# Conditioning tiles on GpSimd's queue, the first scale and shift on TensorE, and six blocks in two halves of k tiles

## Chip, cores and metric

One core of one Trainium2 chip runs the whole kernel in one launch. The metric is device microseconds, lower is better. Engines are named as in the profile: PE is TensorE (matmul), PEld its weight load, DVE is VectorE, ACT is ScalarE, POOL is GpSimd, and SP is SyncE, which here only issues transfers.

## The reference, cut to what matters

```python
def mod(h, shift, scale):        # modulate
    return h * (1 + scale) + shift

c_act = silu(c)                                       # one row of 1024
for i in range(2):
    # 9 rows of 1024 for each layer: shift, scale and gate of three sublayers
    sh0, sc0, g0, sh1, sc1, g1, sh2, sc2, g2 = split(c_act @ mod_w[i] + mod_b[i], 9)
    h = mod(rms_norm(x, norm_g[i, 0]), sh0, sc0)
    x = x + 0.5 * g0 * swiglu(h, ffn_w_gu[i, 0], ffn_w_down[i, 0])
    h = mod(rms_norm(x, norm_g[i, 1]), sh1, sc1)
    x = x + g1 * (pool_mixer(h) if i == 0 else diff_attention(h))
    h = mod(rms_norm(x, norm_g[i, 2]), sh2, sc2)
    x = x + 0.5 * g2 * swiglu(h, ffn_w_gu[i, 1], ffn_w_down[i, 1])
return rms_norm(x, final_g)
```

`x` has 256 tokens of 1024 channels, `w_gu` is 1024 x 5632 (gate and up), `w_down` 2816 x 1024. Everything is float32.

## The kernel before, in words

The channels lie on partitions: `xT` holds `x` as eight k tiles of 128 channels by 256 tokens. There are four FFNs, a pooling mixer after the first and attention after the third.

**Products.** A float32 operand is split into two parts that TensorE takes at its fast rate, `hi` (rounded, ScalarE, L313) and `lo` (the rest, VectorE, L314). Three matmuls, `hi*hi`, `hi*lo` and `lo*hi` (`prod3`, L333 to L335), stand for one product. The activations are split in the same way (`hh`, `hl`). A *weight unit* is 512 rows by 256 columns (512 KB, 24 matmuls); `split_unit` loads it into one of five `raw` buffers from SyncE's queue (L310) and splits it into one of six `hi` and `lo` buffers. `unit()` keeps four units in advance. A *block* is 256 output columns in one PSUM bank: two units.

**Conditioning.** `mod_w` is stored so that a tile of 128 outputs by 1024 inputs (512 KB) is loaded into one of three `cond` buffers, also from SyncE's queue (L268), and VectorE multiplies it with the row `cact` and sums along it (`gemv_tile`, L276). There are 144 such tiles. All but the first 16 are background work: `Background.tick` puts them between the blocks of the FFNs, by the lists `UP` and `DOWN`.

**The start.** The first FFN needs shift and scale of its own sublayer first. The loop takes k tile by k tile: two conditioning tiles give scale and shift of 128 channels, ScalarE and VectorE make `hh` and `hl` of that k tile (L840 to L847), and two narrow units (one k tile of 768 gate columns and one of 768 up columns, 384 KB each) feed it into six blocks that stay open in PSUM, `early`. After eight k tiles the six blocks are complete.

**Order.** Each engine runs its instructions in the order in which the scheduler put them, and so does each issuing queue: a transfer that waits for a buffer holds those behind it. The scheduler picks the order from priorities and its own idea of durations; `issue_after` keeps work behind a given instruction.

At the end of an FFN the residual is added (VectorE, L396), ScalarE squares it, and VectorE sums the squares into `acc` (L407). TensorE needs `acc` (L377) soon after it has begun the next FFN, whose first blocks run on the unnormalised values `xh`, `xl` (L431 to L433).

Of the kernel before, what the change touches and what calls it, by code (L numbers as in the profile page):

```python
# [11 lines left out]
F32 = mybir.dt.float32  # L12
# [23 lines left out]
EARLY = 3  # L36
# [26 lines left out]
def weight_units():  # L63
# [49 lines left out]
def lay_out(inputs):  # L113
# [11 lines left out]
    for name, ix in weight_units():  # L125
# [7 lines left out]
        "c": np.ascontiguousarray(w["c"]),  # L133
        "mod_w": np.ascontiguousarray(w["mod_w"].transpose(0, 2, 1)),
# [8 lines left out]
def trunk(ctx: ExitStack, tc: tile.TileContext, x, c, mod_w, small, weights, diff_lambda, k_rope, out):  # L143
# [72 lines left out]
    for half in range(2):  # L216
        hs = slice(half * KD // 2, (half + 1) * KD // 2)
        nc.sync.dma_start(xT[:, hs, :], x[:, hs, :])
    nc.sync.dma_start(cact, c.broadcast_to([P, D]))
# [7 lines left out]
    warm(AF.Silu, eps1)  # L227
    with tc.high_priority(offset=1000):
        S.activation(cact, cact, AF.Silu)
    warm(AF.Abs_reciprocal_sqrt, cact[:, 0:1])  # L230
# [26 lines left out]
    tiles = iter([(0, p, k) for k in range(KD) for p in (1, 0)] + [(*part, k) for part in PARTS for k in range(KD)])  # L257
    loaded = []

    def gemv_load(n):  # L260
        while len(loaded) < n:
# [6 lines left out]
            nc.sync.dma_start(raw, mod_w[i, r0:r0 + P, :])  # L268
# [33 lines left out]
    place = [0]  # L302

    def split_unit(nk, n):
# [7 lines left out]
        with tc.high_priority(offset=-400):  # L312
            S.activation(hi[:, :w], raw[:, :w], AF.Copy)  # L313
            V.tensor_tensor(lo[:, :w], raw[:, :w], hi[:, :w].bitcast(F32), ALU.subtract)  # L314
# [491 lines left out]
    xr = [t1k(1024, "qk", 2) for _ in range(2)]  # L806
    with tc.high_priority(offset=1000):
        pt = psmall()
        for half in range(2):
            sq = t1k(1024, "u", U_BUFS)  # L810
# [3 lines left out]
        idle = psmall()  # L814
        for _ in range(WARM):
            PE.matmul(idle[:, :P], ones, ones, start=True, stop=True)
# [7 lines left out]
    with tc.high_priority(offset=1000):  # L824
        scaled_x(0, 1)

    early = [psum2(), psum2()] + [psum() for _ in range(2 * EARLY - 2)]
    b1, d = const([P, KD], "b1"), const([P, 2, KD], "d")  # L830
# [5 lines left out]
    def scale_and_shift(k):  # L836
# [89 lines left out]
```

## Time and profile before

| | |
|---|---|
| median of three runs | 946.21 us (945.92 to 951.72) |
| profiled execution | 958.03 us, span of its instructions 956.2 us |
| granted TensorE clock over the span | 0.981 |
| PE / DVE / ACT / POOL busy | 913.8 / 742.8 / 502.4 / 0.7 us |
| transfers | 238.18 MB, mean 249 GB/s; SyncE's queue 236.88 MB of it |

"x" with a number counts instructions, "<-" between names stands between what is written and what is read, and a "<-" in brackets or behind a bar names what ended the idle time. `Lnnn` is a line of the kernel; a helper's line collects the work of all that call it.

### The profile page before, as it was taken

To read this page: it belongs to the slowest core of one execution; us is meant where nothing else is said; L and a number is where in the kernel's file an instruction comes from. 1 tells how busy PE (TensorE), PEld (TensorE's weight loads), DVE (VectorE), ACT (ScalarE), POOL (GpSimd) and SP (SyncE) were. 2 spreads that over 40 slices of the span, in tenths; PEclk is the share of its full clock that TensorE was granted. 3 is DMA by queue.
4 is the path that set the end of the run, shared out by engine and by line. 5 is a ranking of instruction groups with operands and counts; after the bars stand their busy time and mean duration, and the time that the engine had idled before them with its cause. 6 is when DMAs were issued, how large, how long until landed. Compare 5 with 4: busy or idle time off the path is not lost.

```text
span 956.2 us, 18740 instructions
## 1 busy us (share of the span) xinstructions
PE 913.8 (96%) x7532; PEld 900.8 (94%) x7532; DVE 742.8 (78%) x1211; ACT 502.4 (53%) x771; POOL 0.7 (0%) x6
## 2 busy tenths in 40 slices
PE   7999998998989999995999999999999999999997
PEld 6889997998989999985999999999999999999996
DVE  5889888889997787878898877568989896555552
ACT  5574444455654443534564445457777675444541
POOL 0000000000000000000000000000000000000000
PEclk8999999999999999998999999999999999999999
DMA  8989989997559898988778997565543447665531
GB/s 310 323 304 348 360 323 339 350 339 274 191 182 327 313 314 291 333 279 319 248 290 313 324 324 248 177 206 151 162 143 120 155 155 231 187 186 180 176 122 45
DMA packets 68727, 238.18 MB, mean 249 GB/s; under 512 B 7968, under 2 KB 9248, under 8 KB 68640
## 3 DMA queue, kind: packets, MB, share of 16 engines
q1 hardware_dynamic: 68496, 236.88, 72.3%
q8 instruction: 59, 0.97, 0.4%
q14 instruction: 28, 0.23, 0.1%
q10 hardware_dynamic: 144, 0.11, 0.0%
HBM read 234.86 MB, written 1.05 MB: 247 GB/s over the span
## 4 chain that ended last, share of the span: by engine, by line
PE 66%; DMA 13%; DVE 11%; issue 4%; ACT 4%; SPq 1%; DVEq 0%; ACTq 0%
PE mm L335 16%; PE mm L333 16%; PE mm L334 16%; DMA cond<-in_mod_w_dram 12%; DVE lo L314 5%; DVE cond L276 3%; PE mm L431 2%; PE mm L433 2%; PE mm L432 2%; PE hd L333 2%; PE hd L335 2%; PE hd L334 2%; ACT hi L313 2%; DMA raw<-in_weights_dram 1%; PE hd L643 1%
## 5 line engine op out<-in xcount | busy, mean ns | idle before, releaser
L313 ACT ACTIVATE hi<-raw 128x1024 fp32r<-128x1024 f32 (+1 forms) x312 | 315.5, 1023 | 259.2 <-PE mm L334 105.8
L314 DVE TENSOR_TENSOR lo<-raw,hi 128x1024 fp32r<-128x1024 f32 (+1 forms) x312 | 365.5, 1180 | 97.3 <-ACT hi L313 96.5
L335 PE MATMUL mm<-hh,lo 128*128 128x256 f32 x992 | 276.5, 281 | 4.5 <-DVE lo L314 4.5
L333 PE MATMUL mm<-hh,hi 128*128 128x256 f32 x992 | 278.0, 281 | 0.1
L334 PE MATMUL mm<-hl,hi 128*128 128x256 f32 x992 | 277.3, 280 | 0.3 <-DVE hl L421 0.3
L335 PE MATMUL mm<-ahl,lo 128*128 128x256 f32 x768 | 215.5, 281 | 6.7 <-DVE lo L314 6.7
L333 PE MATMUL mm<-ahl,hi 128*128 128x256 f32 x768 | 215.3, 281 | 0.0
L334 PE MATMUL mm<-ahl,hi 128*128 128x256 f32 x768 | 214.9, 280 | 0.0
L276 DVE SCALAR_TENSOR_TENSOR cond<-cond,cact 128x1024 f32<-128x1024 f32 x144 | 174.6, 1221 | 48.6 <-DMA cond<-in_mod_w_dram 47.8
L335 PEld LDWEIGHTS mm<-hh,lo 128*128 128x128 f32 x992 | 186.1, 189 | 6.3 <-DVE lo L314 6.0
L333 PEld LDWEIGHTS mm<-hh,hi 128*128 128x128 f32 x992 | 187.0, 189 | 1.1 <-ACT hi L313 0.3
L334 PEld LDWEIGHTS mm<-hl,hi 128*128 128x128 f32 x992 | 187.2, 189 | 0.5 <-DVE hl L421 0.5
L335 PEld LDWEIGHTS mm<-ahl,lo 128*128 128x128 f32 x768 | 144.8, 189 | 7.7 <-DVE lo L314 7.7
L333 PEld LDWEIGHTS mm<-ahl,hi 128*128 128x128 f32 x768 | 144.8, 189 | 0.3 <-ACT ahl L342 0.2
L334 PEld LDWEIGHTS mm<-ahl,hi 128*128 128x128 f32 x768 | 145.0, 189 | 0.0
L333 PE MATMUL hd<-hh,hi 128*128 128x256 f32 x288 | 81.3, 282 | 5.8 <-ACT hi L313 5.8
L335 PE MATMUL hd<-hh,lo 128*128 128x256 f32 x288 | 81.8, 284 | 3.0 <-DVE lo L314 2.9
L334 PE MATMUL hd<-hl,hi 128*128 128x256 f32 x288 | 81.0, 281 | 0.0
L333 PEld LDWEIGHTS hd<-hh,hi 128*128 128x128 f32 x288 | 54.5, 189 | 6.2 <-ACT hi L313 6.2
L432 PE MATMUL mm<-xl,hi 128*128 128x256 f32 x208 | 60.3, 291 | 0.0
L431 PE MATMUL mm<-xh,hi 128*128 128x258 f32 x208 | 59.0, 290 | 0.8 <-DVE t L516 0.7
L433 PE MATMUL mm<-xh,lo 128*128 128x258 f32 x208 | 59.5, 288 | 0.0
(199 smaller groups left out, 1034.0 us busy)
## 6 DMA issues: line engine op xcount, KB each, us to landing
raw<-in_weights_dram SPq DMA_DIRECT2D x264, 512.0 KB, 4.7
cond<-in_mod_w_dram SPq DMA_DIRECT2D x144, 512.0 KB, 6.2
raw<-in_weights_dram SPq DMA_DIRECT2D x48, 384.0 KB, 5.6
xT<-in_x_dram SPq DMA_DIRECT2D x2, 512.0 KB, 5.0
out_dram<-u SPq DMA_DIRECT2D x4, 256.0 KB, 2.5
cact<-in_c_dram SPq DMA_DIRECT2D x1, 512.0 KB, 7.1
pk<-qk SPq DMA_DIRECT2D x16, 32.0 KB, 3.0
qk<-pk SPq DMA_DIRECT2D x16, 32.0 KB, 1.8
```

What stands on the lines that cost most here:

```text
L276: return V.scalar_tensor_tensor(raw, raw, 1.0, cact, ALU.mult, ALU.mult, accum_out=out)
L313: S.activation(hi[:, :w], raw[:, :w], AF.Copy)
L314: V.tensor_tensor(lo[:, :w], raw[:, :w], hi[:, :w].bitcast(F32), ALU.subtract)
L333: PE.matmul(o, lh, rh, start=start, stop=False, **kw)
L334: PE.matmul(o, lh, rl, start=False, stop=False, **kw)
L335: PE.matmul(o, ll, rh, start=False, stop=stop, **kw)
L431: PE.matmul(o[:, :T + 2], hi[:, kk, cs], xh[:, k, :], start=(k == 0), stop=False)
L432: PE.matmul(o[:, :T], hi[:, kk, cs], xl[:, k, :], start=False, stop=False)
L433: PE.matmul(o[:, :T + 2], lo[:, kk, cs], xh[:, k, :], start=False, stop=(k == KD - 1))
L643: PE.matmul(sc[c2][:, q * T:(q + 1) * T], l[pr, 0, qs], r[pr, 1, :], start=(n == 0), stop=(n == 2))
```

## The change

Three edits come together.

1. `gemv_load` issues the conditioning tiles from GpSimd's queue, except those of the first shift and scale. They keep their three buffers.
2. The first 512 channels of the first scale and shift no longer come from VectorE: TensorE multiplies `c` (its silu, spread over 32 columns, `cwide`) with eight transfers of 512 KB, a new feed `mod_first`, in four strips of 32 output partitions. ScalarE copies the result, TensorE transposes it, and VectorE sums the strips. These transfers use the `raw` buffers. The other four k tiles still take conditioning tiles. The twelve warming matmuls after the statistics are gone.
3. The first FFN's six blocks are computed in two passes over ordinary units: first the k tiles 0 to 3 of all six, then 4 to 7. `EARLY` now counts blocks.

```diff
-EARLY = 3
+EARLY = 6
...
     def ffn(i, s):
-        first = 0
+        blocks = [n * DFF + j * UW for j in range(KF // 2) for n in range(2)]
         if (i, s) == (0, 0):
-            first = EARLY
-            for k in range(KD):
-                for n in range(2):
-                    yield block("ffn_w_gu", (i, s), k * P, (k + 1) * P, n * DFF, n * DFF + EARLY * UW)
-        for j in range(first, KF // 2):
-            for n in range(2):
-                yield from halves("ffn_w_gu", (i, s), n * DFF + j * UW)
+            for half in range(2):
+                for c0 in blocks[:EARLY]:
+                    yield block("ffn_w_gu", (i, s), half * 512, (half + 1) * 512, c0, c0 + UW)
+            blocks = blocks[EARLY:]
+        for c0 in blocks:
+            yield from halves("ffn_w_gu", (i, s), c0)
...
+        "c8": np.ascontiguousarray(w["c"].reshape(P, KD)),
+        "mod_first": np.ascontiguousarray(np.stack([w["mod_w"][0][:, p * D:p * D + 512] for p in (1, 0)])
+                                          .reshape(2, P, 4, 2 * 512).transpose(0, 2, 1, 3)),
...
-    tiles = iter([(0, p, k) for k in range(KD) for p in (1, 0)] + [(*part, k) for part in PARTS for k in range(KD)])
+    tiles = iter([(0, p, k) for k in range(KD // 2, KD) for p in (1, 0)] + [(*part, k) for part in PARTS for k in range(KD)])
...
-            nc.sync.dma_start(raw, mod_w[i, r0:r0 + P, :])
+            (nc.sync if (i, p) in ((0, 0), (0, 1)) else nc.gpsimd).dma_start(raw, mod_w[i, r0:r0 + P, :])
...
-        idle = psmall()
-        for _ in range(WARM):
-            PE.matmul(idle[:, :P], ones, ones, start=True, stop=True)
...
+    def first_gemv(n):
+        pt = psmall()
+        for q in range(4):
+            raw = rawp.tile([P, 1024], F32, tag="raw", name=nm("raw"))
+            nc.sync.dma_start(raw, mod_first[n, q])
+            for k in range(2):
+                kk = 2 * q + k
+                r = kk % 4 * 32
+                PE.matmul(pt[r:r + 32, :], cwide[:, kk, :], raw[:, k * 512:(k + 1) * 512], start=(kk < 4), stop=(kk >= 4),
+                          skip_group_check=True, tile_position=(0, r))
+        row = t1k(512, "qk", 2)
+        S.activation(row, pt, AF.Copy)
+        pt = psmall()
+        for m in range(4):
+            PE.transpose(pt[:, m * P:(m + 1) * P], row[:, m * P:(m + 1) * P], ident)
+        V.tensor_reduce(d[:, 1 - n, 0:4], pt.rearrange("p (m g r) -> p m g r", m=4, g=4)[:, :, :, 0], AX.X, ALU.add)
...
+    with tc.high_priority(offset=500):
+        first_gemv(0)
+        first_scale(0, 4)
+        first_gemv(1)
+        first_shift(0, 4)
+        scaled_x(0, 4)
+        for k in range(4):
+            on_s, on_v = first_norm(k)
+    nc.sync.dma_start(cact, c.broadcast_to([P, D]))
+    early = [psum2(), psum2()] + [psum() for _ in range(EARLY - 2)]
+    with tc.issue_after(on_v):
+        scaled_x(4, 8)
+    for n, pt in enumerate(early):
+        mm_half(pt, 0, hh, hl)
+        if n < 4:
+            k = 4 + n
+            if n == 0:
+                with tc.issue_after(splits[1][0]):
+                    S.activation(cact, cact, AF.Silu)
+            with tc.issue_after(splits[n + 1][1]), tc.issue_after(splits[n + 1][0]):
+                for p in (1, 0):
+                    gemv_tile(0, p, k, d[:, p, k:k + 1])
+                first_scale(k, k + 1)
+                first_shift(k, k + 1)
+                first_norm(k)
+    for pt in early:
+        mm_half(pt, 1, hh, hl)
```

`first_norm` makes `hh` on ScalarE (L871), and `t` and `hl` on VectorE (L872, L873); `first_scale` and `first_shift` are three small VectorE operations (L859, L860, L864). In the changed kernel the conditioning product is L284, its load L276, the weight load L319, `hi` L322, `lo` L323 and the three matmuls L343 to L345.

SyncE's queue at the start, before. `raw` from `weights` is a weight unit, `cond` a conditioning tile:

```order
L218 DMA xT<-in_x_dram 128x1024 x2
L219 DMA cact<-in_c_dram 128x1024
L268 DMA cond_166<-in_mod_w_dram 128x1024
L268 DMA cond_169<-in_mod_w_dram 128x1024
L310 DMA raw_178<-in_weights_dram 128x768
L310 DMA raw_184<-in_weights_dram 128x768
```

The same queue of the changed kernel, from the last two transfers of `mod_first` on:

```order
L844 DMA raw_184<-in_mod_first_dram 128x1024
L844 DMA raw_188<-in_mod_first_dram 128x1024
L884 DMA cact<-in_c_dram 128x1024
L319 DMA raw_226<-in_weights_dram 128x1024
L319 DMA raw_232<-in_weights_dram 128x1024
L319 DMA raw_238<-in_weights_dram 128x1024
L319 DMA raw_244<-in_weights_dram 128x1024
L319 DMA raw_250<-in_weights_dram 128x1024
L276 DMA cond_281<-in_mod_w_dram 128x1024
```

Two conditioning tiles stood ahead of the first weight unit; now eight transfers of `mod_first` and `cact` do, and the first conditioning tile follows five units.

TensorE's order at the start of the changed kernel, from the first transfer of `mod_first` to the first matmul on a weight unit (`st` is a small PSUM tile, `hd` a block's):

```order
L848 MATMUL st_148<-raw_149,cwide_111 32x512 x2
L848 MATMUL st_148<-raw_153,cwide_111 32x512 x2
L848 MATMUL st_148<-raw_157,cwide_111 32x512 x2
L848 MATMUL st_148<-raw_161,cwide_111 32x512 x2
L854 MATMUL st_167<-ident,qk_165 128x128 x4
L848 MATMUL st_175<-raw_176,cwide_111 32x512 x2
L848 MATMUL st_175<-raw_180,cwide_111 32x512 x2
L848 MATMUL st_175<-raw_184,cwide_111 32x512 x2
L848 MATMUL st_175<-raw_188,cwide_111 32x512 x2
L854 MATMUL st_194<-ident,qk_192 128x128 x4
L343 MATMUL hd_219<-hh,hi_227 128x256
```

Before, the first matmul on a weight unit stood right behind the statistics and the warming matmuls; now both products and their transposes stand between.

VectorE's order around the last k tile, before. `hl` is that of k tile 7, `qk` the gated product of a finished block:

```order
L276 SCALAR_TENSOR_TENSOR cond_556,d<-cond_556,cact 128x1024
L847 TENSOR_TENSOR hl<-t_561,hh 128x256
L314 TENSOR_TENSOR lo_603<-raw_601,hi_602 128x768
L314 TENSOR_TENSOR lo_609<-raw_607,hi_608 128x768
L314 TENSOR_TENSOR lo_668<-raw_666,hi_667 128x1024
L503 TENSOR_TENSOR qk_649<-hd_157,qk_649 128x512
L503 TENSOR_TENSOR qk_654<-mm_159,qk_654 128x512
```

And now:

```order
L284 SCALAR_TENSOR_TENSOR cond_417,mod_114<-cond_417,cact 128x1024
L873 TENSOR_TENSOR hl<-t_423,hh 128x256
L284 SCALAR_TENSOR_TENSOR cond_744,mod_114<-cond_744,cact 128x1024
L323 TENSOR_TENSOR lo_429<-raw_427,hi_428 128x1024
L284 SCALAR_TENSOR_TENSOR cond_747,mod_114<-cond_747,cact 128x1024
L284 SCALAR_TENSOR_TENSOR cond_815,mod_114<-cond_815,cact 128x1024
L513 TENSOR_TENSOR qk_667<-hd_220,qk_667 128x512
L284 SCALAR_TENSOR_TENSOR cond_818,mod_114<-cond_818,cact 128x1024
L350 TENSOR_TENSOR ahl<-qk_667,ahl 128x512
L323 TENSOR_TENSOR lo_459<-raw_457,hi_458 128x1024
L284 SCALAR_TENSOR_TENSOR cond_883,mod_114<-cond_883,cact 128x1024
L284 SCALAR_TENSOR_TENSOR cond_886,mod_114<-cond_886,cact 128x1024
```

Those that write `mod` are background tiles. Before, the first of them came after the six blocks' gated products; now they stand between the `lo` of the blocks' second halves.

More of the change, by code (lines that the diff above doesn't have):

```diff
@@ L142, in trunk @@
 @with_exitstack
-def trunk(ctx: ExitStack, tc: tile.TileContext, x, c, mod_w, small, weights, diff_lambda, k_rope, out):
+def trunk(ctx: ExitStack, tc: tile.TileContext, x, c, c8, mod_first, mod_w, small, weights, diff_lambda, k_rope, out):
     nc = tc.nc
@@ L217, in trunk @@
         hs = slice(half * KD // 2, (half + 1) * KD // 2)
[L218 to L219 removed]
+        with tc.high_priority(offset=1000):
+            nc.sync.dma_start(xT[:, hs, :], x[:, hs, :])
+    craw = const([P, KD], "craw")
+    nc.scalar.dma_start(craw, c8)
     vec = {}
@@ L802, in attention @@
                     normalise((j, j + 1), rstd, vecs["A", 1, 1], b)
-    xr = [t1k(1024, "qk", 2) for _ in range(2)]
+    xr = [t1k(1024, "u", U_BUFS) for _ in range(2)]
     with tc.high_priority(offset=1000):
@@ L822, in scaled_x @@
                         rstd.rearrange("p (o t) -> p o t", o=1).broadcast_to([P, n, T]), ALU.mult)
[L824 to L830, printed above, removed]
+    d, b1 = const([P, 2, KD], "d"), const([P, KD], "b1")
     a0 = vecs["A", 0, 0] = const([P, KD], "A00")
@@ L844, in scale_and_shift @@
         with tc.high_priority(offset=100):
-            S.activation(h, xk, AF.Identity, scale=a0[:, ks], bias=sh0[:, ks])
-            second = S.activation(hh[:, k, :], xk, AF.Identity, scale=a0[:, ks], bias=sh0[:, ks])
-            third = V.tensor_tensor(hl[:, k, :], h, hh[:, k, :].bitcast(F32), ALU.subtract)
-        return last.ins, second.ins, third.ins
-    on_v, on_s, after = scale_and_shift(0)
-    for k in range(KD):
-        with tc.issue_after(on_v), tc.issue_after(on_s):
-            prefetch(2)
-            if k < 3:
-                with tc.issue_after(after):
-                    scaled_x(1 << k, 2 << k)
-            if k < KD - 1:
-                on_v, on_s, after = scale_and_shift(k + 1)
-        for h in range(2):
-            hi, lo = ahead.pop(0)
-            for j in range(EARLY):
-                for m in range(2):
-                    cs = slice(j * UW + m * P, j * UW + (m + 1) * P)
-                    pair3(early[2 * j + h], m, hi[:, 0, cs], lo[:, 0, cs], hh[:, k, :], hl[:, k, :], k == 0, k == KD - 1)
+            on_s = S.activation(hh[:, k, :], xk, AF.Identity, scale=a0[:, ks], bias=sh0[:, ks])
+            V.tensor_scalar(h, xk, a0[:, ks], sh0[:, ks], ALU.mult, ALU.add)
+            on_v = V.tensor_tensor(hl[:, k, :], h, hh[:, k, :].bitcast(F32), ALU.subtract)
+        return on_s.ins, on_v.ins
+    with tc.high_priority(offset=500):
[25 more added lines that the diff above has]
+        mm_half(pt, 1, hh, hl)
     ffn(0, 0, 0, ("A", 0, 1), UP[0], DOWN[0], early)
```

27 lines of the change are left out of this document (17 added, 10 removed).

## The prediction

> **What bounds the kernel now.** I read the page's engine line first, then the table of stretches, then the waits of TensorE, and went from each wait to the queue that caused it.
>
> ```profile
> PE 913.8 (96%) x7532; PEld 900.8 (94%) x7532; DVE 742.8 (78%) x1211; ACT 502.4 (53%) x771; POOL 0.7 (0%) x6
> ```
>
> TensorE (PE) is busy for 96% of the span, so time can only be won where it stands still or runs slowly. The table shows where that is. Its columns are the stretch, its length, and for each engine the busy time with the number of instructions in brackets; then the granted TensorE clock, the DMA share and GB/s.
>
> ```profile
> 0.00:60.00 60.00, 49.57 (x348) 47.64 (x349) 41.85 (x70) 35.83 (x60) 0.70 (x6) 0.91 0.89 309
> 60.00:140.00 80.00, 78.86 (x663) 78.04 (x662) 71.49 (x99) 38.26 (x46) 0.00 (x0) 1.00 0.93 345
> 140.00:180.00 40.00, 34.33 (x274) 33.12 (x273) 33.66 (x51) 19.73 (x25) 0.00 (x0) 0.96 0.95 345
> 180.00:220.00 40.00, 40.00 (x342) 40.00 (x341) 36.09 (x56) 18.25 (x26) 0.00 (x0) 1.00 0.92 327
> 220.00:280.00 60.00, 53.95 (x412) 51.97 (x412) 55.27 (x117) 35.44 (x62) 0.00 (x0) 0.94 0.59 197
> 280.00:420.00 140.00, 140.00 (x1191) 140.00 (x1190) 113.50 (x160) 62.61 (x78) 0.00 (x0) 1.00 0.90 312
> 420.00:460.00 40.00, 27.88 (x207) 27.08 (x206) 32.41 (x53) 15.79 (x22) 0.00 (x0) 0.83 0.89 312
> 460.00:640.00 180.00, 180.00 (x1528) 179.96 (x1527) 141.27 (x209) 93.05 (x119) 0.00 (x0) 1.00 0.77 266
> ```
>
> From 460 to 640 us nothing is missing: 1528 matmuls in 180 us, 0.118 us each. Measured by that rate, 19.0 us are lost before 60 (60 - 348 x 0.118), 1.9 from 60 to 140, 7.7 from 140 to 180, 11.5 from 220 to 280 (the pooling mixer) and 15.6 from 420 to 460. About 12 more lie behind 640, so some 67 us of the 956 are lost in all. The change touches the first three stretches directly, and the fifth through the queue.
>
> ```profile
> PE mm L335 <- DVE lo L314: 11.2, 10, 3.2
> PE st L377 <- DVE acc L407: 10.0, 1, 10.0
> PE hd L333 <- ACT hi L313: 5.8, 2, 4.1
> ```
>
> The largest single wait, 10.0 us, stands at the end of the second FFN, where L377 needs the sum of squares that VectorE (DVE) writes. The timeline of VectorE shows why it was late there, and why not at the like place one FFN later (the last row):
>
> ```profile
> 441.68 1.23 DVE L276 SCALAR_TENSOR_TENSOR cond<-cond,cact 128x1024 f32<-128x1024 f32 x1 [2.31 <-DMA cond<-in_mod_w_dram]
> 442.93 1.22 DVE L276 SCALAR_TENSOR_TENSOR cond<-cond,cact 128x1024 f32<-128x1024 f32 x1
> 444.08 1.22 DVE L314 TENSOR_TENSOR lo<-raw,hi 128x1024 fp32r<-128x1024 f32 x1
> 445.29 1.22 DVE L314 TENSOR_TENSOR lo<-raw,hi 128x1024 fp32r<-128x1024 f32 x1
> 449.25 0.87 DVE L396 SCALAR_TENSOR_TENSOR xT<-mm,G,xT 128x256 f32<-128x256 f32 x2
> ...
> 639.62 0.87 DVE L396 SCALAR_TENSOR_TENSOR xT<-mm,G,xT 128x256 f32<-128x256 f32 x2
> ```
>
> At 442 VectorE still works off conditioning tiles that landed late, and the residual (L396) stands behind them until 449. At 640 there are no such tiles left, and TensorE waits for nothing. Two answers on VectorE's waits, the first for 280 to 460 and the second for 60 to 220, tell how far that reaches:
>
> ```profile
> DVE cond L276 <- DMA cond<-in_mod_w_dram: 28.7, 22, 3.8
> DVE cond L276 <- DMA cond<-in_mod_w_dram: 1.2, 2, 0.6
> ```
>
> So late conditioning tiles cost VectorE 28.7 us ahead of the big wait, and almost nothing before 220, where VectorE is simply full (71.5 of 80 us). They are late because SyncE issues everything in one order:
>
> ```profile
> 140.14 0.33 SPq L268 DMA_DIRECT2D cond<-in_mod_w_dram  x1
> 140.56 1.23 SPq L310 DMA_DIRECT2D raw<-in_weights_dram  x2
> 141.88 4.35 SPq L268 DMA_DIRECT2D cond<-in_mod_w_dram  x2
> 146.32 0.86 SPq L310 DMA_DIRECT2D raw<-in_weights_dram  x2
> ...
> SPq L310 <- DVE lo L314: 444.8, 212, 10.1
> SPq L268 <- DVE cond L276: 105.6, 42, 5.7
> ```
>
> A conditioning load holds the next weight load for 4.35 us here, and elsewhere weight loads that wait for `lo` hold conditioning loads.
>
> **The change, part by part.** *Queue.* 128 of the 144 conditioning loads go to GpSimd's queue, which has nothing else (0.70 us busy). A load then starts when its buffer is free. The trace shows no GpSimd load; its price is bounded below by nothing, since the same bytes move, and above by the landing time at which it holds VectorE up (second rival). I take the median of SyncE's loads:
>
> ```profile
> cond<-in_mod_w_dram SPq DMA_DIRECT2D x144, 512.0 KB, 6.2
> ```
>
> Three buffers at 6.2 us and 1.15 us of work each give a tile every 2.5 us; the down projections need 16 tiles in 62 us. The 28.7 us of waits go, VectorE reaches L396 in time, and of the 15.6 us lost from 420 to 460 I credit 12: the 10.0 and 2 for the clock, which is 0.83 there. Late next are the `lo` that TensorE already waits for, so the remaining 3.6 stay.
>
> *First scale and shift.* These rows price the start:
>
> ```profile
> 6.32 3.72 PE L813 MATMUL st<-u,ones 128*128 128x256 f32 x16 [0.65 <-ACT u L811]
> 9.88 2.84 PE L816 MATMUL st<-ones 128*128 128x128 f32 x24
> 16.86 0.58 PE L333 MATMUL hd<-hh,hi 128*128 128x256 f32 x1 [4.14 <-ACT hi L313]
> L674 PE MATMUL st<-ident,u x32: 270/273/273, 671.4 to 737.4; 128*128 128x128 f32 x32
> L497 ACT ACTIVATE qk<-mm x37: 572/580/602, 59.6 to 880.0; 128x512 f32<-128x512 f32 x37
> L846 ACT ACTIVATE hh<-qk,mod,A x8: 583/588/592, 15.5 to 54.7; 128x256 fp32r<-128x256 f32 x8
> L313 ACT ACTIVATE hi<-raw 128x1024 fp32r<-128x1024 f32 (+1 forms) x312 | 315.5, 1023 | 259.2 <-PE mm L334 105.8
> ```
>
> Today TensorE starts on the weights at 16.86, since the first k tile needs only two conditioning tiles. After the change it needs all eight transfers of `mod_first` and 16 float32 matmuls of 512 columns. A float32 matmul is two passes in the trace (8 matmuls of L813, 16 records), and those 16 take 3.72 us: 0.22 us per 256 columns, hence 0.44 per pass of 512 and 1.77 per transfer, which brings two matmuls. Eight transfers at 309 GB/s take 1.7 us each, so TensorE and the transfers go in step, and TensorE ends at about 9.9 + 8 x 1.77 = 24.1. The transposes of the first product stand between the two halves in TensorE's order, and hold it for a ScalarE copy (0.58) and eight passes of 128 columns (0.11 each, half of a 256): 1.5. A second copy, transposes and the sums on VectorE take another 1.9: 27.5. Then ScalarE makes four `hh` at about 0.5 apart and the first `hi` (1.02), and TensorE starts at 30.5, 13.6 us later than now. The twelve warming matmuls (L816) are gone; they cover the wait at 9.9 to 12.7, where TensorE now has work. The strips of 32 columns sit in no row of this trace. If two of them ran side by side, the products would take half, 7 us less; the nearest rows, the float32 matmuls of L813, run one behind the other, so I take the serial end.
>
> By the Trainium skill's page "TensorE: Matmul & The Clock Gate", Part 3, matmuls on different column strips run at once (three strips of 32 columns: 2.38 times as fast). No row here shows it; by that page the start would be some 7 us shorter, and the time about 937.
>
> *Halves, and VectorE's order.* The six blocks have the same 288 matmuls before and after. The first halves can be fed early, but the second halves need `hl` of k tile 7, and in VectorE's new order ahead of it stand, after the first four tiles: 8 `lo` (1.15 us apart by the rows at 442 to 445), 8 late conditioning tiles and 2 of the background (1.15 each), 4 pairs of `t` and `hl`, and 12 single columns.
>
> ```profile
> 26.48 0.43 DVE L847 TENSOR_TENSOR hl<-t,hh 128x256 fp32r<-128x256 f32 x1 [0.62 <-ACT hh L846]
> 26.82 1.22 DVE L821 TENSOR_TENSOR qk<-xT,pk 128x1024 f32<-128x1024 f32 x1
> ...
> 9.88 1.28 ACT L212 ACT_TABLE_LOAD   x1
> ```
>
> From 27.5: eight small operations at 0.34 and `scaled_x` at 1.2 give 31.4; then 9.2 + 11.5 + 2.7 + 1.8 = 25.2, and 1.3 for the table load that now precedes `cact` and holds the third `hi`: 58. The TensorE order has 24 matmuls of the second halves ahead of that point, so 120 remain, 14.1 us; and VectorE has six more background tiles and four `lo` to do in that time (11.5, and 2.3 of other work), with `lo` of the last unit at 72 and its 21 matmuls behind it. The six blocks end at about 75 or 76, against 60 now (348 less 64 warming and statistics matmuls are 284 of 288). That is **16 us later**. Were the strips side by side, everything moves 7 up, 9 later.
>
> This loss buys something: by the first block after the six, VectorE has 15 background tiles behind it instead of 3, 12 x 1.15 = 14 us of work and 12 transfers. The stretches from 60 to 180, which lose 1.9 + 7.7 because VectorE and the queue are full, should then lose nothing: credit **9.6**. Costed at nothing: ScalarE loses 16 tiny and 8 `t` activations, hidden under TensorE; if ScalarE were on the path they would be worth a few us early. `cact` moves behind `mod_first` (1.7 us of transfer, under the products); uncovered, it delays the first unit by as much.
>
> **Sum.** In the profiled execution's terms: 958.0 + 16 - 9.6 - 12 = 952.4. That execution is 11.8 us longer than the median of the runs, 946.2, so the runs lose some 55 us where the trace loses 67, and the credits, which are waits, hold there at 55/67 = 0.82: 17.7 of 21.6. The start is engine work and counts in full. **946.2 + 16 - 17.7 = 944.5 us**, no change that can be told; 1% either way is about what a measurement of this kernel can tell from none.
>
> **Rivals.** *Strips at once and credits in full.* The start costs 9, and the whole 25.2 of the two stages comes back: 930. For it speaks that TensorE lost nothing at 640; against it that the runs already have fewer waits than the trace. It also decides the low end.
>
> *Conditioning tiles become the bound: slower.* Behind the six blocks VectorE's order has two conditioning tiles ahead of every two `lo`. A pair of blocks is 96 matmuls, 11.3 us, with four tiles, one per 2.8 us; three buffers allow 8.5 us per round, 7.3 from freed buffer to landing. If GpSimd's loads land later than 7.3 us, TensorE waits for every `lo` behind them. At 8.5 us the round is 9.65, 0.4 us per tile, over the 24 or so that are left of the first up projection's 32 about 9.5 us, and the credit from 60 to 180 is gone: 946.2 + 16 + 9.5 - 0.82 x 12 = 962. SyncE's median of 6.2 speaks against it.
>
> *The queue buys nothing.* If SyncE's weight loads, not its order, make the tiles late, only VectorE's lead counts: 946.2 + 16 - 0.82 x 9.6 = 954. Against it stand the 105.6 us in which SyncE stood at conditioning loads for VectorE. The Trainium skill's page "DMA: Bandwidth & Descriptors", section "Rules for kernel authors", says that spreading loads over issuing engines does not help bandwidth and saves only issue time; by that rule this case holds.
>
> **How the numbers follow.** Forecast 0.45 (937 to 950), first rival 0.25, second 0.18, third 0.12. Faster by over 1% (under 936.7): the first rival and 0.05 of the forecast, 0.30. Slower by over 1% (over 955.7): the second rival and 0.03 of the third, 0.21. Within 1%: 0.49. The range runs from the first rival's 930 to the second's 962, which is the spread of the unknown prices: strips 7, queue 0 to 12, landing up to 8.5 us.
>
> **What would show it.** Right: the first matmul on `hi` at about 30, the last of the six blocks at about 75, a gap of TensorE before the `hl` of tile 7, no wait at L377's successor near 450, landings of GpSimd's loads near 6 us. Wrong: a first matmul before 25 (strips at once), background tiles on VectorE that wait for loads by several us each (second rival), or the 10 us wait still there (third). If the six blocks end before 65, my reading of VectorE's order failed.

## The result, and the profile after

The changed kernel takes **1006.2 us** (median of 4 runs, 1002.6 to 1012.0), the kernel before 948.3 on the same chip: a ratio of 1.061 (95% interval 1.055 to 1.068). Forecast were 944.5 us, in a range up to 962. The profiled execution spans 1009.8 us, 53.6 more than that of before.

First the engines, then the stretches of the prediction's table, with the same columns:

```profile
PE 943.7 (93%) x7548; PEld 921.7 (91%) x7548; DVE 737.8 (73%) x1215; ACT 491.0 (49%) x745; POOL 68.4 (7%) x134
```

```profile
0.00:60.00 60.00, 45.60 (x275) 36.94 (x276) 36.07 (x76) 25.43 (x32) 4.00 (x12) 0.89 0.89 327
60.00:140.00 80.00, 72.86 (x581) 71.36 (x581) 67.66 (x98) 32.41 (x39) 14.24 (x27) 0.98 0.92 333
140.00:180.00 40.00, 39.15 (x327) 38.95 (x326) 35.83 (x53) 18.24 (x22) 6.87 (x13) 1.00 0.95 349
180.00:220.00 40.00, 34.96 (x275) 34.35 (x274) 31.16 (x48) 14.97 (x20) 6.87 (x13) 0.96 0.89 317
220.00:280.00 60.00, 43.72 (x321) 41.97 (x322) 52.84 (x95) 23.38 (x37) 9.50 (x18) 0.86 0.87 317
280.00:420.00 140.00, 132.57 (x1080) 131.23 (x1079) 118.28 (x196) 62.88 (x89) 17.94 (x34) 0.99 0.80 277
420.00:460.00 40.00, 34.25 (x253) 33.05 (x254) 31.49 (x50) 14.72 (x21) 6.86 (x13) 0.91 0.88 307
460.00:640.00 180.00, 177.41 (x1459) 176.54 (x1458) 119.35 (x167) 92.99 (x120) 2.11 (x4) 0.99 0.63 203
```

Stretches that were full have holes now: 280 to 420 has 1080 matmuls where before had 1191, 180 to 220 has 275 for 342. GpSimd's column shows its loads in every stretch to 460 and almost none after: all conditioning tiles are done by then. VectorE has 119.35 us of work left in 460 to 640, where before had 141.27.

The waits of TensorE, then VectorE's waits for conditioning tiles in 280 to 460 and in 60 to 220 us (the two windows that the prediction used), then the loads with KB and the median time to landing:

```profile
PE mm L345 <- DVE lo L323: 25.8, 23, 3.2
PE st L394 <- DVE acc L417: 12.4, 1, 12.4
PE hd L343 <- ACT hi L322: 5.6, 3, 3.5
PE hd L343 <- ACT hh L871: 4.3, 1, 4.3
...
DVE cond L284 <- DMA cond<-in_mod_w_dram: 29.0, 15, 3.3
DVE cond L284 <- DMA cond<-in_mod_w_dram: 21.5, 15, 3.1
```

```profile
raw<-in_weights_dram SPq DMA_DIRECT2D x276, 512.0 KB, 4.5
cond<-in_mod_w_dram POOLq DMA_DIRECT2D x128, 512.0 KB, 6.5
```

The wait for `lo` rose from 11.2 to 25.8 us. VectorE's wait for conditioning tiles did not fall with their own queue: 29.0 us late in the kernel, where before had 28.7, and 21.5 us early, where before had 1.2. The 10 us wait at the end of the second FFN (L387 now) is gone, but 12.4 us stand at L394, where the pooling mixer begins, and GpSimd's loads, all issued between 43 and 467 us, wait for a free buffer for most of that time:

```profile
POOL cond L276 <- DVE cond L284: 385.2, 121, 42.0
```

VectorE's timeline at L394 has the very picture that the prediction read at 442 us of the kernel before, one FFN earlier:

```profile
252.84 1.23 DVE L284 SCALAR_TENSOR_TENSOR cond<-cond,cact 128x1024 f32<-128x1024 f32 x1 [1.25 <-DMA cond<-in_mod_w_dram]
...
256.71 1.22 DVE L284 SCALAR_TENSOR_TENSOR cond<-cond,cact 128x1024 f32<-128x1024 f32 x1 [1.50 <-DMA cond<-in_mod_w_dram]
257.86 0.08 DVE L284 DVE_READ_ACCUMULATOR cond<-cond,cact 128x1 f32 x1
257.86 1.22 DVE L323 TENSOR_TENSOR lo<-raw,hi 128x1024 fp32r<-128x1024 f32 x1
259.00 1.22 DVE L284 SCALAR_TENSOR_TENSOR cond<-cond,cact 128x1024 f32<-128x1024 f32 x1
260.14 0.08 DVE L284 DVE_READ_ACCUMULATOR cond<-cond,cact 128x1 f32 x1
260.14 1.22 DVE L323 TENSOR_TENSOR lo<-raw,hi 128x1024 fp32r<-128x1024 f32 x1
261.28 0.87 DVE L406 SCALAR_TENSOR_TENSOR xT<-mm,G,xT 128x256 f32<-128x256 f32 x2
```

The residual (L406) stands behind tiles that land late, TensorE behind the residual, and the clock falls to 0.86 there.

Two more things differ. The order of the program on VectorE has moved far more than the 12 tiles that the prediction counted. This table gives the number of conditioning tiles ahead of the nth `lo` in it (the new start needs 8 tiles and 4 `lo` fewer; the last two columns are `start_alone` and `after_paced`, below):

| nth `lo` | before | after | after, queue SP | after, paced |
|---|---|---|---|---|
| 17 | 16 | 22 | 10 | 8 |
| 73 | 64 | 79 | 58 | 56 |
| 97 | 74 | 91 | 67 | 62 |
| 129 | 98 | 130 | 93 | 78 |

And TensorE's step from one matmul to the next, where nothing waits, is 120.0 ns in all of the changed kernel, against 117.8 in most of before. The stretch 840 to 900 us of both, TensorE's busy time first (before, then after):

```profile
840.00:900.00 60.00, 60.00 (x512) 60.00 (x511) 32.16 (x32) 28.24 (x33) 0.00 (x0) 1.00 0.58 178
840.00:900.00 60.00, 60.00 (x502) 60.00 (x501) 34.29 (x34) 28.20 (x33) 0.00 (x0) 1.00 0.64 203
```

There is no conditioning tile left at that point, the granted clock is 1.00 in both, and still 512 matmuls have become 502. Over 7548 matmuls 2.2 ns would be 17 us.

### The profile page after: what moved, and what is told of

It reads as the page before. It is cut to its first block, busy times and chain, and to the rows that moved or that the text cites. A ratio compares the mean times of both kernels' runs of the same rounds, so it can differ in the third digit from the quotient of the medians.

```text
span 1009.8 us, 18822 instructions
## 1 busy us (share of the span) xinstructions
PE 943.7 (93%) x7548; PEld 921.7 (91%) x7548; DVE 737.8 (73%) x1215; ACT 491.0 (49%) x745; POOL 68.4 (7%) x134
## 4 chain that ended last, share of the span: by engine, by line
PE 53%; issue 34%; POOL 6%; DMA 3%; DVE 2%; ACT 1%; POOLq 0%; SPq 0%; DVEq 0%; ACTq 0%
PE mm L343 13%; PE mm L345 13%; PE mm L344 13%; POOL cond L276 6%; DMA cond<-in_mod_w_dram 2%; PE mm L441 2%; PE mm L443 2%; PE mm L442 2%; PE hd L345 2%; PE hd L344 2%; PE hd L343 2%; PE hd L653 1%; DVE cond L284 1%; PE st L703 1%; DMA raw<-in_mod_first_dram 1%
## 5 line engine op out<-in xcount | busy, mean ns | idle before, releaser
L322 ACT ACTIVATE hi<-raw 128x1024 fp32r<-128x1024 f32 (+1 forms) x308 | 314.8, 1034 | 317.8 <-PE mm L344 130.0
L323 DVE TENSOR_TENSOR lo<-raw,hi 128x1024 fp32r<-128x1024 f32 (+1 forms) x308 | 365.4, 1193 | 139.4 <-ACT hi L322 138.6
L345 PE MATMUL mm<-hh,lo 128*128 128x256 f32 x992 | 282.9, 286 | 8.9 <-DVE lo L323 8.9
L343 PE MATMUL mm<-hh,hi 128*128 128x256 f32 x992 | 282.0, 285 | 2.9 <-ACT qk L507 2.9
L345 PE MATMUL mm<-ahl,lo 128*128 128x256 f32 x768 | 221.2, 288 | 16.9 <-DVE lo L323 16.9
L344 PE MATMUL mm<-ahl,hi 128*128 128x256 f32 x768 | 220.1, 287 | 1.2 <-DVE ahl L350 1.2
L343 PE MATMUL mm<-ahl,hi 128*128 128x256 f32 x768 | 220.1, 287 | 0.0
L284 DVE SCALAR_TENSOR_TENSOR cond<-cond,cact 128x1024 f32<-128x1024 f32 x136 | 164.9, 1219 | 63.4 <-DMA cond<-in_mod_w_dram 63.4
L345 PEld LDWEIGHTS mm<-hh,lo 128*128 128x128 f32 x992 | 191.0, 193 | 11.5 <-DVE lo L323 11.1
L343 PEld LDWEIGHTS mm<-hh,hi 128*128 128x128 f32 x992 | 191.4, 193 | 3.8 <-ACT qk L507 3.1
L345 PEld LDWEIGHTS mm<-ahl,lo 128*128 128x128 f32 x768 | 149.8, 195 | 19.8 <-DVE lo L323 19.8
L344 PEld LDWEIGHTS mm<-ahl,hi 128*128 128x128 f32 x768 | 150.0, 195 | 1.5 <-DVE ahl L350 1.4
L343 PEld LDWEIGHTS mm<-ahl,hi 128*128 128x128 f32 x768 | 149.9, 195 | 0.3 <-DVE xT L406 0.2
L276 POOL DMA_DIRECT2D cond<-in_mod_w_dram x128 | 67.7, 529 | 399.0 <-DVE cond L284 385.2
L343 PE MATMUL hd<-hh,hi 128*128 128x256 f32 x288 | 83.5, 290 | 9.9 <-ACT hi L322 5.6
L345 PE MATMUL hd<-hh,lo 128*128 128x256 f32 x288 | 82.9, 289 | 1.4 <-DVE lo L323 1.4
L343 PEld LDWEIGHTS hd<-hh,hi 128*128 128x128 f32 x288 | 56.7, 197 | 10.8 <-ACT hi L322 6.3
L349 ACT ACTIVATE ahl<-qk 128x512 fp32r<-128x512 f32 x40 | 24.9, 622 | 81.1 <-DVE qk L513 81.1
```

The costliest lines, as they stand in the source:

```text
L276: (nc.sync if (i, p) in ((0, 0), (0, 1)) else nc.gpsimd).dma_start(raw, mod_w[i, r0:r0 + P, :])
L284: return V.scalar_tensor_tensor(raw, raw, 1.0, cact, ALU.mult, ALU.mult, accum_out=out)
L322: on_s = S.activation(hi[:, :w], raw[:, :w], AF.Copy)
L323: on_v = V.tensor_tensor(lo[:, :w], raw[:, :w], hi[:, :w].bitcast(F32), ALU.subtract)
L343: PE.matmul(o, lh, rh, start=start, stop=False, **kw)
L344: PE.matmul(o, lh, rl, start=False, stop=False, **kw)
```

## Experiments: which part costs

Each time stands beside runs of the kernel before on the same chip (948 to 953 us by group of runs).

**Queue alone** (`q_alone`), **start alone** (`start_alone`), **the changed kernel paced** (`after_paced`), and the kernel before once more (`before_again`, unchanged).

```diff
 q_alone, against before
-            nc.sync.dma_start(raw, mod_w[i, r0:r0 + P, :])
+            (nc.sync if (i, p) in ((0, 0), (0, 1)) else nc.gpsimd).dma_start(raw, mod_w[i, r0:r0 + P, :])
 start_alone, against after
-            (nc.sync if (i, p) in ((0, 0), (0, 1)) else nc.gpsimd).dma_start(raw, mod_w[i, r0:r0 + P, :])
+            nc.sync.dma_start(raw, mod_w[i, r0:r0 + P, :])
 after_paced, against after (in gemv_steps; splits[-1][1] is the lo of the newest weight tile)
-            gemv_tile(i, p, k, mod[i][:, p * KD + k:p * KD + k + 1])
+            with tc.issue_after(splits[-1][1]):
+                gemv_tile(i, p, k, mod[i][:, p * KD + k:p * KD + k + 1])
```

> The kernel before with one edit: the conditioning tiles, but for those of the first scale and shift, are issued from GpSimd's queue. The start is that of the kernel before. Theory 1 (VectorE's order): the loss of the change behind the start, 11 us between the 1000th and the 2000th matmul and 9 us between the 2500th and the 3500th, comes from the order that the queue brings, in which VectorE has done 134 conditioning tiles ahead of its 129th lo and the kernel before 98; it expects these 20 us here, so 968 us, and 985 us if the longer step from one matmul to the next (120.0 ns after, 117.8 ns before) comes with the queue as well. Theory 2 (the start): what the change lost behind the start follows from its later start, and the queue alone gains, as predicted, the waits of the kernel before: 930 us.

Measured: **992.0 us**, ratio 1.044 (1.036 to 1.051). The loss comes with the queue alone, with the old start. It is twice the 20 us that theory 1 had for this case, at a step of 117.8 ns.

> The changed kernel with all conditioning tiles on SP's queue again: the new start alone. Theory 1 (VectorE's order, brought by the queue): the 19 us of the start stay and the 20 us behind it go, about 967 us, with 93 conditioning tiles ahead of VectorE's 129th lo. If the longer step between matmuls (120.0 ns) belongs to the start's code, 983 us; if it belongs to the queue, the step is 117.8 ns here. Theory 2 (all from the start): as slow as the changed kernel, 1000 us or more.

Measured: **962.5 us**, ratio 1.014 (1.007 to 1.022). The loss behind the start is gone with the queue, as theory 1 said, but the longer step is not: it belongs to the new start's kernel (120.0 ns). Theory 1 had 983 us for that case, 20 too many. Against the kernel before, 43 us of loss come with the queue and 13 with the new start's kernel.

> The changed kernel, in which each conditioning tile of the background is ordered on VectorE behind the lo of the newest weight tile (78 tiles ahead of the 129th lo in place of 130); the queue stays GpSimd's. Theory 1 (VectorE's order): the 20 us of loss at 180 to 475 us go, about 986 us, and the wait of TensorE for lo in 380 to 475 us (15.6 us in the changed kernel) falls below 4 us. Theory 2 (landing): the loss comes from the tiles of GpSimd's queue, which land 6.5 us after their issue instead of 4.8 us on three buffers; then the order changes nothing, the waits for lo stay and the time stays within 5 us of 1006 us.

Measured: **944.4 us**, ratio 0.994 (0.991 to 0.998). The 20 us expected were 62. What the edit moves is the place of the conditioning products in VectorE's order, and with it when the loads are released; the scheduler shifted some other instructions along with them, some 2% of TensorE's matmuls among them. Landing by itself is no explanation: the tiles of the kernel before landed 6.2 us after their issue, not 4.8 as theory 2 had it, against 6.5 in the changed kernel. The same queue, the same loads; the waits for `lo` by the main matmuls have left the list (of TensorE's waits above 1 us only those of the start are left):

```profile
PE hd L344 <- ACT hi L323: 6.2, 3, 3.5
PE st L849 <- DMA raw<-in_mod_first_dram: 1.1, 3, 0.7
PE mm L200 <- DVE eps L203: 1.1, 1, 1.1
```

The same stretches, paced: each is full, and GpSimd still loads in 460 to 640, where the changed kernel had long finished.

```profile
180.00:220.00 40.00, 40.00 (x336) 40.00 (x335) 35.30 (x55) 18.93 (x25) 5.30 (x10) 1.00 0.95 349
220.00:280.00 60.00, 59.68 (x490) 58.99 (x490) 55.37 (x115) 40.36 (x68) 1.06 (x2) 1.00 0.53 183
280.00:420.00 140.00, 140.00 (x1169) 140.00 (x1169) 109.83 (x148) 65.66 (x81) 15.37 (x29) 1.00 0.85 292
420.00:460.00 40.00, 40.00 (x333) 39.74 (x332) 35.32 (x70) 24.15 (x36) 1.06 (x2) 1.00 0.67 226
460.00:640.00 180.00, 180.00 (x1499) 179.74 (x1498) 149.96 (x223) 89.75 (x113) 21.20 (x40) 1.00 0.87 303
```

> The kernel before, unchanged, for the step from one matmul to the next on this chip: 117.8 ns between 800 and 935 us if the 120.0 ns of the changed kernel belong to that kernel; 120.0 ns here, or in some of these kernels without a rule, if they belong to the execution or the chip.

Measured: a single run, 948.4 us; 117.8 ns to 632 us with few exceptions, and 113.3 ns from 786 us on (532 matmuls from 840 to 900, where the other execution of the same kernel had 512). So neither branch held as written: the step can differ between executions of one kernel, but 120.0 ns all through came only with the new start.

**Is it the pacing or the queue** (`q_paced`: the kernel before with both edits above, and the list `splits` for the second; `sync_paced`: the changed kernel paced, all tiles on SP's queue)?

> The kernel before with the conditioning tiles of the background on GpSimd's queue and, on VectorE, each behind the lo of the newest weight tile: its start is the old one. If the order on VectorE is the whole of what the queue costs, the paced queue is worth here what it is worth to the new start (944.4 against 962.5 us, 18 us): 949 - 18 = 931 us, and 50 us or more under the same kernel without the pacing (992 us). If the pacing helps only together with the new start, it stays between 945 and 992 us.

Measured: **925.7 us**, ratio 0.973 (0.968 to 0.979): 66 us under the queue without pacing, 24 under before.

> The changed kernel with the pacing on VectorE and all conditioning tiles on SP's queue. If the 18 us between the new start alone (962.5 us) and the changed kernel paced (944.4 us) come from the order on VectorE, this runs at about 944 us too, and GpSimd's queue is worth nothing; if they come from the queue, as the prediction had it (17.7 us), it stays near 962 us.

Measured: **960.6 us**, ratio 1.012 (1.006 to 1.018). The queue is worth 16.2 us, once it is paced; the pacing on SP's queue is worth 1.9 (962.5 to 960.6). The reason stands in SP's waits of `sync_paced`: a conditioning load that waits for its buffer holds the weight loads behind it.

```profile
SPq L320 <- DVE lo L324: 367.4, 192, 9.8
SPq L276 <- DVE cond L284: 199.9, 112, 5.7
```

**Why does that order cost so much: VectorE's time, or bytes?** `half_bytes` keeps the changed kernel's order and loads half of each background tile; it leaves out the other half of the sum, so its modulation vectors are not the reference's. `full_bytes` is its control (the same buffers, whole loads, no factor).

```diff
 half_bytes, against after
...
-            raw = rawp.tile([P, D], F32, tag="cond", name=nm("cond"), bufs=COND_BUFS)
+            raw = cbufs[place_c[0] % COND_BUFS]
+            place_c[0] += 1
...
+                nc.gpsimd.dma_start(raw[:, :512], mod_w[i, r0:r0 + P, :512])
...
-        return V.scalar_tensor_tensor(raw, raw, 1.0, cact, ALU.mult, ALU.mult, accum_out=out)
+        return V.scalar_tensor_tensor(raw, raw, 1.0 if (i, p) in ((0, 0), (0, 1)) else 0.25, cact, ALU.mult, ALU.mult, accum_out=out)
```

> The changed kernel with its order on VectorE (130 conditioning tiles ahead of the 129th lo), but only the first half of each conditioning tile of the background is loaded, 256 KB in place of 512; VectorE multiplies and sums the whole tile as before, over what the second half held, and by a factor of 0.25 more, so these modulation vectors are others. Three fixed buffers stand in place of the pool's three. Theory D (the order hurts because it asks the DMA engines for weights and tiles together faster than they bring them: in 380 to 475 us they are 85 to 91% busy and VectorE waits 20.9 us for tiles there): the waits for lo go and the time falls by most of what the pacing brought (62 us), to 945 to 965 us. Theory V (VectorE's own time for tiles ahead of lo, 1.22 us each): within 10 us of 1006 us.

> The same with whole tiles and without the factor, that is the changed kernel with three fixed buffers in place of the pool's: 1006 us within 8 us by both theories, so that the difference to the run with half the bytes is that of the bytes.

Measured: **961.2 us** with half the bytes (ratio 1.011, 1.006 to 1.016), 1005.7 (a single run) with all. The 180 to 280 and 380 to 475 us of the control, then of half the bytes:

```profile
180.00:280.00 100.00, 79.37 (x606) 76.42 (x605) 86.10 (x148) 41.43 (x64) 15.84 (x30) 0.91 0.87 313
380.00:475.00 95.00, 81.48 (x628) 78.78 (x627) 76.89 (x119) 33.57 (x45) 15.83 (x30) 0.96 0.89 317
...
180.00:280.00 100.00, 94.03 (x750) 92.76 (x750) 95.12 (x180) 53.11 (x84) 13.50 (x26) 0.97 0.69 227
380.00:475.00 95.00, 94.76 (x782) 93.89 (x781) 85.50 (x149) 50.26 (x74) 8.58 (x16) 1.00 0.72 240
```

With the same order TensorE is full in the later stretch (94.76 of 95). So some 45 of the 62 us are the bytes. The other 16 to 17, by which `half_bytes` is still above `after_paced`, lie where VectorE has products ahead of more urgent work: set beside the paced trace, 6.0 us are lost up to the 500th matmul and 8.9 between the 1500th and the 1750th, where the pooling mixer begins. That they are VectorE's own time is argued, not shown, since VectorE still waits 15.2 us for tiles in `half_bytes`.

The arithmetic of the bytes: a weight tile is 24 matmuls, 2.88 us at 120.0 ns, and 0.524 MB, 182 GB/s. Between the 97th and the 129th `lo` the changed order has 39 conditioning tiles per 32 weight tiles: 2.22 times 182 is 404 GB/s to keep TensorE fed. The stretches of the changed kernel up to 460 us moved 277 to 349, and the fastest stretch of `q_paced` (180 to 220 us, DMA share 1.00) 386. The kernel before has 24 tiles there, 1.75 times 185 (at 117.8 ns), 324 GB/s, which its row for 280 to 420 (312 GB/s, 0.90 busy) just holds.

The Trainium skill's page "DMA: Bandwidth & Descriptors", section "Where 436 GB/s comes from", gives memory about 358 GB/s for one core (716 over two). The traces do not show it as a bound here, where one core runs: the 386 GB/s above exceed it, and 404 lies above both.

The bytes can make tiles late in a second way, by the round of the three buffers. Per tile the order asks for one every 2.4 us (32 x 2.88 / 39), while three buffers, with a landing of 6.5 us and 1.2 us of work, give one every 2.6. With half the bytes a tile lands after 4.3 us (6.2 in the control), so `half_bytes` eases the rate of the DMA engines and the round at once. No run has more buffers; which of the two binds first stays open.

## Experiments: TensorE's step

Do the 32-column strips leave TensorE slower, or is it where the tiles lie? `before_strips` puts strips into the old start, `one_strip` takes them out of the new one.

```diff
 before_strips, against before
-    for _ in range(WARM):
-        PE.matmul(pt[:, :P], ones, ones, start=True, stop=True)
+    for n in range(WARM):
+        r = n % 4 * 32
+        PE.matmul(pt[r:r + 32, :P], ones[:, :32], ones, start=True, stop=True, skip_group_check=True, tile_position=(0, r))
 one_strip, against after_paced
-                PE.matmul(pt[r:r + 32, :], cwide[:, kk, :], raw[:, k * 512:(k + 1) * 512], start=(kk < 4), stop=(kk >= 4),
-                          skip_group_check=True, tile_position=(0, r))
+                PE.matmul(pt[0:32, :], cwide[:, kk, :], raw[:, k * 512:(k + 1) * 512], start=(kk == 0), stop=(kk == 7))
...
```

> The kernel before, whose first 12 warming matmuls (their results are not used) are done with 32 columns of weights in one of four column strips. Theory S (the strips leave TensorE in a longer step): 120.0 ns from one matmul to the next between 860 and 925 us and nearly all through, as in every kernel with the new start so far. Theory L (something else of the new start, the places of the tiles in memory among it): 117.8 or 113.3 ns, as in the kernels with the old start.

> The changed kernel paced, in which all eight k tiles of the first scale and shift add up in one strip of 32 columns without a column position, so that no two of these matmuls lie beside each other. Theory S: 117.8 ns or less from one matmul to the next behind the start, and some 16 us less over the whole kernel, while the first main matmul comes later than 24.7 us. Theory L: 120.0 ns all through, and a time some us above that of the kernel paced (944 us).

(The lines left out at the end copy, transpose and pick the result from 32 partitions in place of 128.) Measured, a single run each: 951.4 us with 117.8 and 113.3 ns; 949.0 us with 120.0 ns all through. Theory S is out. `one_strip` also prices the strips, in TensorE's timeline of the products (a record is one of the two passes of a matmul); first one transfer's two matmuls of the changed kernel and its first main matmul, then the second product and first main matmul in one strip:

```profile
18.70 1.05 PE L848 MATMUL st<-raw,cwide 128*32 128x512 f32 x4 [0.24 <-DMA raw<-in_mod_first_dram]
24.68 0.58 PE L343 MATMUL hd<-hh,hi 128*128 128x256 f32 x1 [3.51 <-ACT hi L322]
...
18.31 7.05 PE L848 MATMUL st<-raw,cwide 128*32 128x512 f32 x16
30.71 0.79 PE L344 MATMUL hd<-hh,hi 128*128 128x256 f32 x2 [2.42 <-ACT hh L870]
```

A record takes 0.26 us in strips and 0.44 in one strip, and the strips wait for transfers: the first main matmul comes 6.0 us earlier.

What else moved with the new start is memory: its small constants shift the weight tiles (`hi`, `lo`) by 64 bytes per partition, from 160 to 224 bytes past a multiple of 256, while `hh`, `hl` and `ahl`, which the matmuls stream, stay at 224. The remaining runs only put bytes in (N is 16, 24, 32, 48 floats: 64, 96, 128, 192 bytes; `q_paced_aligned` has N = 16 and 32 bytes ahead of `xT` as well):

```diff
     cact = const([P, D], "cact")
+    V.memset(const([P, N], "pad"), 0.0)
```

> The kernel before, queue and pacing as in the 925.7 us version, with 64 bytes per partition put in ahead of the pools, so that every hi and lo tile lies at the byte where the changed kernel has it (224 bytes past a multiple of 256 in place of 160; hh, hl and ahl do not move). Theory A (the place of the weight tiles in memory sets TensorE's step): 120.0 ns from one matmul to the next between 860 and 905 us and nearly all through, as in every kernel with the new start, and 15 to 20 us more, about 943 us. Theory B (something else of the new start): 117.8 ns and 926 us.

> The changed kernel paced, with 192 bytes per partition put in, so that the weight tiles lie 160 bytes past a multiple of 256 as in the kernel before. Theory A: 117.8 ns or less between matmuls and 15 to 20 us less, about 927 us. Theory B: 120.0 ns and 944 us.

> As the first, with 96 bytes: the weight tiles begin at a multiple of 256 bytes, hh, hl and ahl stay 224 past one. Theory A: the step is another than 117.8 ns, if the alignment of the weight tiles counts a shorter one (113.3 ns, the shortest in these traces: 7,500 times 4.5 ns, 34 us less, about 892 us); if it is only a matter of the distance between the tiles, none can be said. Theory B: 117.8 ns and 926 us.

> As the third, with 32 bytes put in ahead of xT as well: weight tiles and hh, hl, ahl all begin at a multiple of 256 bytes. Theory A: if both operands' places count, at least as fast as the third; if only the weight tiles' place counts, the same step as there. Theory B: 117.8 ns and 926 us.

> The kernel before, queue and pacing, with 128 bytes put in: the weight tiles 32 bytes past a multiple of 256, hh, hl and ahl 224 past one. So far the step between matmuls was 120.0 ns with both operands at the same residue (224 and 224, 0 and 0), 117.8 ns with 64 between them (160 and 224) and 118.3 ns with 0 and 224. If any distance but none gives about 117.8 ns, 926 us here; if the distance of 64 is the only good one, 118.3 to 120.0 ns and 928 to 937 us.

> As that with 192 bytes: weight tiles 96 past a multiple of 256 and 128 away from hh, hl and ahl. If the step falls with the distance up to the half of 256 bytes, it is shorter here than 117.8 ns, at best 113.3 ns, and the time 895 to 926 us; if any distance does, 926 us; if 64 is the only good one, 928 to 937 us.

Measured, with the step in undisturbed stretches after 100 us (mean of start to start):

| kernel | weights, past 256 | streamed, past 256 | step, ns | us | ratio to before (95%) |
|---|---|---|---|---|---|
| `q_paced` | 160 | 224 | 117.8 | 925.7 | 0.973 (0.968 to 0.979) |
| `q_paced_pad64` | 224 | 224 | 120.0 | 937.3 | 0.983 (0.979 to 0.988) |
| `after_paced` | 224 | 224 | 120.0 | 944.4 | 0.994 (0.991 to 0.998) |
| `after_paced_pad192` | 160 | 224 | 117.8 | 933.3 | 0.979 (0.975 to 0.983) |
| `q_paced_aligned` | 0 | 0 | 120.0 | 938.3 | 0.984 (0.980 to 0.988) |
| `q_paced_pad96` | 0 | 224 | 118.3 | 928.5 | 0.974 (0.970 to 0.979) |
| `q_paced_pad128` | 32 | 224 | 113.3 and 117.8 | 913.4 | 0.960 (0.955 to 0.966) |
| `q_paced_pad192` | 96 | 224 | 120.0 and 118.7 | 933.0 | 0.982 (0.978 to 0.985) |

The same stretch as above for the first, second, fourth and seventh of them, in that order; the first count in brackets is that of TensorE's matmuls:

```profile
840.00:900.00 60.00, 60.00 (x512) 60.00 (x511) 32.00 (x36) 29.44 (x39) 0.00 (x0) 1.00 0.48 152
840.00:900.00 60.00, 60.00 (x502) 60.00 (x501) 33.15 (x39) 28.58 (x37) 0.00 (x0) 1.00 0.59 178
840.00:900.00 60.00, 60.00 (x512) 60.00 (x511) 32.81 (x38) 28.41 (x36) 0.00 (x0) 1.00 0.56 172
840.00:900.00 60.00, 60.00 (x530) 59.84 (x529) 28.81 (x35) 26.74 (x37) 0.00 (x0) 1.00 0.39 128
```

Theory A holds in both directions: 64 bytes make the old start's kernel slow (512 to 502 matmuls, +11.6 us), 192 bytes make the new start's fast (502 to 512, -11.2 us), and nothing else of the new start is needed for it. (The runs stem from different chips; with each beside the kernel before of its own group, the two differences are +8.8 and -14.6.) It is not the alignment of either operand but how they lie to each other: equal residues gave 120.0 ns twice, at 224 and at 0. The rules that I tried for the rest failed: with 32 against 224 the step is the shortest, where I expected no more than 117.8, and with 96, half of 256 away, it is nearly the longest. The runs do not settle that 256 is the right modulus: modulo 128, 160 and 32 are the same place, and 117.8 and 113.3 ns occur with both (`before_again` has 160), while 96 is then the place of 224, and shows 120.0 ns for part of its time.

Last, the best place found on two other kernels, the kernel before and the changed kernel paced (the same line with 32 and 16 floats):

> The kernel before with nothing changed but 128 bytes put in, so that the weight tiles lie 32 bytes past a multiple of 256, as in the fastest version so far (913.4 us against 925.7 us, 12 us for these bytes). If the place of the tiles is worth the same without queue and pacing: 951 - 12 = 939 us; if the faster step only makes VectorE and the transfers late, no more than 3 us less than before.

> The changed kernel paced, with 64 bytes put in: the same place of the weight tiles, 32 past a multiple of 256, with the new start. If place and start add up: 913.4 + 6.7 (the new start's part between the two paced kernels with equal places) = 920 us, with a step of 113.3 ns in some stretches; if the 113.3 ns come only with the old start, 117.8 ns or more throughout and 933 us.

Measured: `before_pad128` **944.8 us**, ratio 0.992 (0.989 to 0.995), between the two expectations: 113.3 ns in over a third of its 941 us, and part of the gain given back. `after_paced_pad64` **919.8 us** (four runs from 912.0 to 932.1, a wide spread), ratio 0.961 (0.955 to 0.967), as expected by the sum, with 113.3 ns in several stretches.

The fastest version is `q_paced_pad128`, 913.4 us: old start, GpSimd's queue, pacing, 128 bytes.

## Why the prediction was wrong, point by point

The pieces, each from a pair of medians: the order on VectorE under the queue +61.8 us (1006.2 against 944.4); the place of the weight tiles +11.2 (944.4 against 933.3); the new start +7.6 (933.3 against 925.7); the queue together with the pacing -24.1 (925.7 against 949.8). They add up to +56.5, and measured were +57.9; since each pair begins where the one before it ends, they must, and the sum confirms nothing. Each is good to a few us, since the medians of the kernel before lay between 948.3 and 952.7 in these groups of runs; set beside the kernel before of their own groups, the place is +14.6 and the new start +4.7.

- **"This loss buys something", credit 9.6: the step that failed.** The prediction saw that VectorE's order takes 12 background tiles early and booked it as a lead. It looked no further than the first block behind the six, asked in its forecast only for VectorE's time, and not for the loads. The order goes on taking tiles ahead, to 130 before the 129th `lo` where before had 98, and asks for one every 2.4 us between the 97th and the 129th, if TensorE is to be kept busy; the prediction's own figure for three buffers was one every 2.5. So VectorE's waits for tiles, which the prediction had gone, are there (29.0 us late, 21.5 early), and the `lo` behind those tiles come late. A credit of 9.6 was a loss of 61.8, some 45 of it the tiles' bytes.
- **Credit 12 at 420 to 460.** The mechanism was right, and its condition was not met. In the paced kernel the stretch is full (40.00 of 40), the wait at the second FFN's end gone, and the queue worth 16.2 us on the new start, and 24.1 with the pacing on the old, where 17.7 were forecast for both credits together. In the changed kernel as it stands the wait moved to the end of the FFN before, to L394, and grew to 12.4.
- **Start, +16.** The six blocks end at 76.5 us, forecast 75 to 76, but by other parts, so the agreement is luck. The strips do run side by side, so the first main matmul comes at 24.7 and not 30.5, as the Trainium skill's page "TensorE: Matmul & The Clock Gate", Part 3, has it for strips (0.26 against 0.44 us a record here, two strips at a time, since each transfer feeds two; its 2.38 times is for three). Then the conditioning tiles ahead of the second halves give the gain back, with a wait of 4.3 us for `hh` of k tile 7. Paced, the six blocks end at 67.8, and at equal places the new start costs 6.7 us of trace, 7.6 of the medians: half of the term at most. It wins nothing back behind it.
- **Not in the sum: where the tiles lie.** +11.2 us, from 64 bytes of new constants. Nothing in the trace of before announces it, except that its step is not constant either.
- **Rivals.** The first had the strips right and the credits wrong. The second, tiles as the bound, was the right kind. It was priced for one projection (9.5 us) and by a landing time over 7.3 us, from a tile per 2.8 us. At the 2.4 us that the order came to ask for, three buffers allow 5.9 us (3 x 2.4 less 1.2 of work, unrounded), and the median of 6.5 is over that; the loss ran through the first and the second FFN. It was held up by SyncE's median of 6.2, a number of the old order. The third, the queue buys nothing, is out by `sync_paced`; the rule that stood with it, from the Trainium skill's page "DMA: Bandwidth & Descriptors", section "Rules for kernel authors" (spreading loads over issuing engines does not help bandwidth), is not touched, since what the queue bought was that the weight loads no longer wait behind a conditioning load.

## What to carry to other kernels

A load that gets a queue of its own also gets a new place in the order of the engine that uses it: look at that order to its end, and work out the bytes per microsecond that it asks for before a lead is booked as a gain. Background work wants to be tied to the pace of the work that it lies beside; here one edge per tile turned a loss of 4% into a gain of 3% on the old start (0.973), and a loss of 6% into a time within 1% of before on the new (0.994). After a change in small constants, compare the step of undisturbed matmuls before and after: a few bytes of padding were worth more than the new start cost.

## What was not expected of the hardware

The step between matmuls of 256 columns at a granted clock of 1.00 took steady values from 113.3 to 120.0 ns, depending on the places of weights and streamed operand (given here modulo 256 bytes); with equal residues it was 120.0 in all undisturbed stretches of the FFNs. With other distances it can change within a run and between executions of the same kernel (117.8 in one, 113.3 in another from 840 to 900 us). Why, the modulus, and the rule for the best distance stay open: five distances were tried, and the pads move the buffers of VectorE, ScalarE and the transfers as well, so that it is TensorE's own two reads that meet is only argued.

The Trainium skill's page "TensorE: Matmul & The Clock Gate", section "Wait — 56ns, not 53.3ns?", gives the columns over 2.4 GHz plus about 2.5 ns between matmuls, 109.2 ns for 256 columns as an estimate from it. No run here reached it; the shortest step was 113.3 ns.
